# Differential attention with streamed weights: weight splits ordered behind an exponential, and two key tiles moved ahead of a hold

## The chip, the cores and the metric

One core of a Trainium2 chip runs the whole program. The metric is the device time of one execution in microseconds (us). Engines: PE (TensorE) multiplies matrices, DVE (VectorE) and ACT (ScalarE) do elementwise work, POOL (GpSimd) does small powers and issues some DMAs, SP issues the weight loads.

## The reference

The program is two transformer blocks in float32 on 1024 tokens of width 1024. The change touches one stage, the differential attention of the second block: 8 heads, each with two score maps, 64-wide queries and keys, 128-wide values, a mask that is causal by chunks of 64 tokens, and queries in blocks of 128.

```python
q = rope_partial(rms_norm(q, q_norm), cos, sin) * (ATTN_HEAD_DIM ** -0.5)
k = rope_partial(rms_norm(k, k_norm), cos, sin)
for blk in range(s // Q_BLOCK):
    q0, q1 = blk * Q_BLOCK, (blk + 1) * Q_BLOCK
    sc = jnp.einsum('bqhmd,bkhmd->bhmqk', q[:, q0:q1], k[:, :q1])
    mask = (jnp.arange(q1) // CHUNK_2)[None, :] <= (jnp.arange(q0, q1) // CHUNK_2)[:, None]
    p = jax.nn.softmax(jnp.where(mask, sc, NEG_INF), axis=-1)
    w = p[:, :, 0] - lam * p[:, :, 1]
    outs.append(jnp.einsum('bhqk,bkhd->bqhd', w, v[:, :q1]))
```

The same stage also multiplies the normed input by the key, value and query weights, and by two gate weights whose tanh goes to memory.

## The kernel before

**Precision.** Every matmul operand in float32 is split into a high and a low part (`split`, L168: an ACT copy makes the high part, a DVE subtraction the low part), and `mm3` (L171) multiplies high by high, high by low and low by high.

**Weights.** `stream` (L1150) brings one piece of weight of 128x1024: a DMA on SP into a raw buffer (a ring of 2), then the split into one of 4 pairs of buffers (`wh`, `wl`). `w2` (L1216) streams two pieces, which hold one head pair's 256 columns of the key, value or query weight. `gate_w` (L1272) streams one piece for a gate; a gate piece serves two gate units.

**Units.** The heads go in four pairs (p). A pair has 16 units (`units`, L1420), in the order of query tiles 0, 7 for one head, 0, 7 for the other, then 1, 6, then 2, 5, then 3, 4; I number them 0 to 15. The last unit of a pair, number 15, is query tile 4 of the second head. `unit_qk` (L1481) computes the scores and their two exponentials (L1522, tile `e`, recorded on the helper's line 154); `unit_mix` (L1526) combines the two maps on DVE; `unit_tr` transposes the result and splits it (`wth`, `wtl`); `unit_pv` multiplies by the values. Scores of tiles 4 to 7 need two PSUM buffers of the tag `sc`, scores of tiles 0 to 3 one; there are two such buffers.

**Fillers.** Between the units' steps the program puts work of its own that feeds later units. `fillers` (L1352) is a generator: for each pair `k_tiles` (8 key tiles and 8 value tiles), then 8 query tiles and gate units between them, and at the end two more gate units. A projected tile (`proj`, L1219) is 24 matmuls in four steps of a nominal 0.65 us, a gate unit eight such steps. `fill(us)` advances the generator until the nominal time is used; `need` (L1409) advances it until a query tile is there. A yield of a pair such as `("k", p)` is a hold: the generator stands still until the loop adds it to `done`. The hold on keys is lifted when the last unit of the pair before is the current one (L1445), the hold on values after that unit's product (L1467).

**PSUM of projections.** `proj` takes the one buffer of the tag `pj`, but inside `need` (`alone`) two of three projections take an `sc` buffer instead.

**Order on the engines.** Every engine runs its own queue in order. A compile-time scheduler writes these queues: it takes instructions by priority, which is the order in which the Python code emits them, but lets a later one go first when an engine would stand idle by the scheduler's own model of time and buffers. So fillers run earlier in the queues than their place in the code. `issue_after(ins)` adds an edge that holds only for the order: what the block emits on the engine of `ins` stands behind `ins` in that queue. Waits on data are separate.

Of the kernel before, what the change touches and what calls it, by code (L numbers as in the profile page):

```python
# [16 lines left out]
AF = mybir.ActivationFunctionType  # L17
# [112 lines left out]
class Model:  # L130
# [906 lines left out]
    def lru(self):  # L1037
        nc, A = self.nc, self.A
        D = self.dram
        self.ghb = [D.tile([128, 1024], F32, name=f"gh{i}") for i in range(8)]  # L1040
        self.tab = [D.tile([128, 1024], F32, name=f"ta{i}") for i in range(16)]
        self.x0 = None
        self.w4p = self.pool("w4")
        W = self.w4 = self.w4p.__enter__()
        self.at0p = self.pool("at0")
        self.at0 = self.at0p.__enter__()
        with self.pool("lru") as T, self.pool("m2") as M, \
# [47 lines left out]
            for c in range(8):  # L1095
# [3 lines left out]
                ps = [*proj()][1]  # L1099
# [11 lines left out]
                for g, t in ((1, ti), (0, tr)):  # L1111
                    for h in range(2):
                        z = slice(h * 512, h * 512 + 512)
                        p = PG.tile([128, 512], F32, name="pg", tag="pg")
# [84 lines left out]
    def attention(self):  # L1199
        nc, A = self.nc, self.A  # L1200
        self.ob = [self.dram.tile([128, 1024], F32, name=f"ob{i}") for i in range(8)]
        self.t0b = [self.dram.tile([128, 1024], F32, name=f"t0{i}") for i in range(8)]
        W = self.w4
        with self.pool("at1") as T1, self.pool("at") as T, \
# [8 lines left out]

            alone = [False, 0]

            def w2(src):  # L1216
                return [self.stream(W, src[j], [128, 4, 256]) for j in range(2)]

            def proj(w, i, out):  # L1219

                alone[1] = (alone[1] + 1) % 3
                if alone[0] and alone[1]:
                    p2 = PS.tile([128, 256], F32, name="pj", tag="sc")
                else:
                    p2 = PJ.tile([128, 256], F32, name="pj", tag="pj")
                q = slice(i * 128, i * 128 + 128)
                for k in range(8):
                    c = w[k // 4]
                    self.mm3(p2, (self.xnh[:, k, q], self.xnl[:, k, q]), (c[0][:, k % 4], c[1][:, k % 4]),
                             k == 0, k == 7)  # L1230
                    if k % 2:
                        yield 0.65
                c = T0.tile([128, 4, 64], F32, name="pc", tag="pc", bufs=2)
                self.act(c.rearrange("p a b -> p (a b)"), p2, AF.Copy)
                out.append(c)

            def norm_rope(ps, i, is_k):

                d = T1.tile([128, 4, 2, 64], F32, name="nr", tag="nr", bufs=3)
                sq = T0.tile([128, 4, 64], F32, name="nq", tag="nq", bufs=1)  # L1240
                self.act(sq, ps, AF.Square)
                ss = T0.tile([128, 8], F32, name="ss", tag="ss", bufs=8)
                if not is_k:
                    self.act(d, ps[:, :, None, :].to_broadcast([128, 4, 2, 64]), AF.Copy)
                nc.vector.tensor_reduce(out=ss[:, 0:4], in_=sq, op=OP.add, axis=AX.X)
                self.ts(ss[:, 0:4], ss[:, 0:4], 1.0 / 64, OP.mult, EPS, OP.add)
                self.rsqrt(ss[:, 4:8], ss[:, 0:4], 4)
                if is_k:
                    self.tt(d, ps[:, :, None, :].to_broadcast([128, 4, 2, 64]),
                            ss[:, 4:8, None, None].to_broadcast([128, 4, 2, 64]), OP.mult)  # L1250
                s = d[:, :, 0]
                r = T1.tile([128, 2, 4, 16], F32, name="rp", tag="rp", bufs=1)
                tb = rot[int(is_k)][:, i]
                for j in range(2):
                    self.tt(r[:, j].rearrange("p a (b c) -> p a b c", b=2),
                            s[:, :, None, 8 * j:8 * j + 8].to_broadcast([128, 4, 2, 8]),
                            tb[:, j:j + 1].rearrange("p a (b c) -> p a b c", b=2).to_broadcast([128, 4, 2, 8]),
                            OP.mult)
                self.tt(d[:, :, :, 0:16], r[:, 0, :, None, :].to_broadcast([128, 4, 2, 16]),
                        r[:, 1, :, None, :].to_broadcast([128, 4, 2, 16]), OP.add)  # L1260
                return d, ss[:, 4:8]
# [8 lines left out]
            gst = {}  # L1270

            def gate_w(j):  # L1272
                if j < 16 and j not in gst:
                    g, n = gates[j]
                    gst[j] = self.stream(W, A["w_gl2" if g == 0 else "w_ga2"][n], [128, 8, 128])

            def gate_unit(u):
                j, h = divmod(u, 2)
# [17 lines left out]
            WQ = {}  # L1296

            def k_tiles(p):
                wk = w2(A["w_k2"][p])
                wv = w2(A["w_v2"][p])  # L1300
                yield "k", p
                kh = T.tile([128, 4, 1024], F32R, name="kh", tag="kh")
                kl = T.tile([128, 4, 1024], F32R, name="kl", tag="kl")
                V = T.tile([128, 8, 2, 2, 128], F32R, name="V", tag="V")
                KV[p] = [kh, kl, V]
                pend = []

                def finish():
                    j, d = pend.pop(0)
                    pt = transposed(d)  # L1310
                    q = slice(j * 128, j * 128 + 128)
                    self.act(kh[:, :, q], pt, AF.Copy, scale=gcol[:, 1:2])
                    self.stt(kl[:, :, q], pt, gcol[:, 1:2], kh[:, :, q].bitcast(F32), OP.mult, OP.subtract)

                for n in range(8 + 2):
                    if n < 8:
                        o = []
                        yield from proj(wk, n, o)
                        d, _ = norm_rope(o[0], n, True)
                        pend.append((n, d))  # L1320
                    if n == 1:
                        yield "v", p
                    if n > 1:
                        j = n - 2
                        o = []
                        yield from proj(wv, j, o)
                        ps = o[0].rearrange("p (h a) b -> p h (a b)", h=2)
                        self.split(V[:, j, :, 0], V[:, j, :, 1], ps)
                        finish()
                        yield 0.3  # L1330
                        if j == 3:
                            WQ[p] = w2(A["w_q2"][p])

            def q_tile(p, i):
                o = []
# [145 lines left out]
    def unit_qk(self, unit, QS, KV):  # L1481
        nc = self.nc
        T, PS, PT, _, ma, mb, lamn, _ = self.at
        p, i, hh = unit
        self.mark(f"at{p}.{i}.{hh}")
        qs, rq = QS[p, i]
        kh, kl, _ = KV[p]
        W = (i + 1) * 128
        wc = max(W, 256)
        one = wc <= 512  # L1490
        pieces = [(0, wc)] if one else [(0, wc // 2), (512, wc // 2)]
        st = T.tile([128, 8], F32, name="st", tag="st", bufs=3)
        rqh = rq[:, 2 * hh:2 * hh + 2]
        es, vs = [], []
        sc = None
        for m in range(2):
            a = 2 * hh + m
            if m == 0 or not one:
                sc = PS.tile([128, 2, 512], F32, name="sc", tag="sc")
            base = sc[:, m] if one else sc.rearrange("p a b -> p (a b)")  # L1500
            k0 = 0
            for pi, (o, n) in enumerate(pieces):
                last = pi == len(pieces) - 1
                nc.tensor.matmul(base[:, o:o + n], qs[:, a], kh[:, a, k0:k0 + n], start=True, stop=False)
                nc.tensor.matmul(base[:, o:o + n], qs[:, a], kl[:, a, k0:k0 + n], start=False, stop=not last)
                if last:

                    end = 128 if i == 0 else o + n
                    nc.tensor.matmul(base[:, end - 64:end], ma, mb, start=False, stop=True)
                k0 += n  # L1510
            if not one:
                v = sc[:, :, 0:W // 2]
                nc.vector.tensor_reduce(out=st[:, m:m + 1], in_=v, op=OP.max, axis=AX.XY)
                self.stt(st[:, m:m + 1], st[:, m:m + 1], -1.0, rqh[:, m:m + 1], OP.mult, OP.mult)
            vs.append(sc[:, m, 0:W] if one else v)
        if one:
            nc.vector.tensor_reduce(out=st[:, 0:2], in_=sc[:, :, 0:W], op=OP.max, axis=AX.X)
            self.stt(st[:, 0:2], st[:, 0:2], -1.0, rqh, OP.mult, OP.mult)
        for m in range(2):
            e = T.tile([128, 512 if one else 1024], F32, name="e", tag=f"e{m}{int(one)}", bufs=1)  # L1520
            ev = e[:, 0:W] if one else e[:, 0:W].rearrange("p (a b) -> p a b", a=2)
            self.act(ev, vs[m], AF.Exp, bias=st[:, m:m + 1], scale=rqh[:, m:m + 1], accum=st[:, 2 + m:3 + m])  # L1522
            es.append(e[:, 0:W])
        return {"st": st, "es": es, "i": i, "hh": hh, "po": None}

# [1028 lines left out]
```

## Time and profile before

| | us |
|---|---|
| median of 3 runs | 2488.14 |
| lowest, highest | 2485.55, 2493.98 |
| the profiled execution | 2485.62 |
| its span, first to last instruction | 2483.9 |

The attention stage runs from about 703 us to 1440 us of the span. Its four pairs repeat one pattern with a period of about 179.5 us; the first pair is followed here, whose last unit ends at 882 us. The profiled execution lies 2.5 us below the median; 1.7 us of it lie outside its span.

### The profile page before, as it was taken

The numbers are of one execution on the slowest core, as the hardware profiler recorded it, in microseconds if no ns is written. First come the engines' busy times: TensorE is split into PE (matmuls) and PEld (weight loads), VectorE is DVE, ScalarE is ACT, GpSimd is POOL, SyncE is SP. The second block draws the span as 40 slices with busy tenths as digits, with TensorE's granted clock in tenths as the row PEclk, the third lists the DMA queues.
The fourth block names the chain that finished last, engine by engine and source line by source line (L and its number), as shares of the span: only waits on it lengthen the run. The fifth ranks groups of instructions, "written<-read, shape, count | busy, mean of one in ns | idle before, by whom it ended". The sixth has DMA issues, their size and how long they took to land. (4 is left out here: it accounts for less than half of the span.)

```text
span 2483.9 us, 35045 instructions
## 1 busy us (share of the span) xinstructions
PE 2355.6 (95%) x13016; PEld 1936.7 (78%) x13016; DVE 1748.2 (70%) x3344; ACT 1314.5 (53%) x2102; POOL 341.5 (14%) x363
## 2 busy tenths in 40 slices
PE   8999989999999999999899899999997999999998
PEld 6888868787888898798798678887885777666765
DVE  9667767677875666666666744235667999898987
ACT  5344532445645455454445432134435888787886
POOL 1011114100021021121121100000011111111111
PEclk9999999999999999999999999999998999999999
DMA  6322353322221111110111456532267999999992
GB/s 222 99 68 67 117 179 127 123 78 84 72 77 39 64 45 42 51 52 35 56 51 40 144 199 221 176 119 77 85 244 271 368 376 373 371 372 359 368 371 66
DMA packets 103838, 394.32 MB, mean 159 GB/s; under 512 B 14129, under 2 KB 33073, under 8 KB 79089
## 3 DMA queue, kind: packets, MB, share of 16 engines
q1 hardware_dynamic: 85008, 335.18, 37.5%
q0 software_dynamic: 18656, 56.88, 7.3%
q8 instruction: 104, 1.70, 0.3%
q14 instruction: 70, 0.57, 0.1%
HBM read 339.07 MB, written 61.31 MB: 161 GB/s over the span
## 5 line engine op out<-in xcount | busy, mean ns | idle before, releaser
L166 DVE TENSOR_TENSOR wl<-raw,wh 128x1024 fp32r<-128x1024 f32 (+1 forms) x496 | 587.7, 1209 | 130.3 <-ACT wh L154 126.1
L154 ACT ACTIVATE wh<-raw 128x1024 fp32r<-128x1024 f32 (+1 forms) x496 | 512.1, 1048 | 250.0 <-PE pj L174 67.2
L173 PE MATMUL pj<-wh,xnh 128*128 128x256 f32 x768 | 222.2, 289 | 2.1 <-ACT tg L154 1.0
L175 PE MATMUL pj<-wh,xnl 128*128 128x256 f32 x768 | 217.2, 283 | 0.0
L174 PE MATMUL pj<-wl,xnh 128*128 128x256 f32 x768 | 217.0, 283 | 0.0
L175 PE MATMUL pg<-wh,xl 128*96 128x512 f32 x512 | 201.3, 393 | 1.6 <-DVE xl L166 1.6
L174 PE MATMUL pg<-wl,xh 128*96 128x512 f32 x512 | 202.6, 396 | 0.0
L173 PE MATMUL pg<-wh,xh 128*96 128x512 f32 x512 | 200.2, 400 | 0.9 <-ACT xh L154 0.9
L173 PEld LDWEIGHTS pj<-wh,xnh 128*128 128x128 f32 x768 | 145.4, 189 | 3.8 <-ACT pc L154 2.5
L174 PEld LDWEIGHTS pj<-wl,xnh 128*128 128x128 f32 x768 | 145.2, 189 | 0.0
L175 PEld LDWEIGHTS pj<-wh,xnl 128*128 128x128 f32 x768 | 145.1, 189 | 0.0
L154 ACT ACTIVATE e<-sc,st,ss 128x1024 f32<-128x1024 f32 (+7 forms) x128 | 105.7, 829 | 54.2 <-DVE st L158 42.4
L178 POOL TENSOR_TENSOR ss<-ss,mhalf 128x4 f32<-128x4 f32 (+1 forms) x68 | 72.7, 1069 | 343.5 <-DVE ss L163 318.4
L173 PE MATMUL pd<-wh,ah 128*96 128x512 f32 x248 | 98.2, 400 | 16.6 <-ACT y L154 16.6
L175 PEld LDWEIGHTS pg<-wh,xl 128*96 128x96 f32 x512 | 83.1, 162 | 38.6 <-DVE xl L166 3.2
L173 PEld LDWEIGHTS pg<-wh,xh 128*96 128x96 f32 x512 | 83.0, 162 | 33.8 <-ACT xh L154 1.3
L174 PEld LDWEIGHTS pg<-wl,xh 128*96 128x96 f32 x512 | 82.8, 162 | 32.4
L173 PE MATMUL pg<-xnh,wh 128*128 128x512 f32 x256 | 104.9, 410 | 0.4 <-ACT kv L154 0.2
L175 PE MATMUL pg<-xnh,wl 128*128 128x512 f32 x256 | 102.6, 401 | 0.0
L173 PE MATMUL pj<-xnh,wh 128*128 128x512 f32 x256 | 102.2, 400 | 0.0
L174 PE MATMUL pg<-xnl,wh 128*128 128x512 f32 x256 | 102.2, 399 | 0.0
L174 PE MATMUL pj<-xnl,wh 128*128 128x512 f32 x256 | 101.2, 396 | 0.0
(998 smaller groups left out, 6327.5 us busy)
## 6 DMA issues: line engine op xcount, KB each, us to landing
raw<-in_w_gu SPq DMA_DIRECT2D x128, 1024.0 KB, 15.3
raw<-in_w_dn SPq DMA_DIRECT2D x64, 1024.0 KB, 15.9
raw<-in_w_out SPq DMA_DIRECT2D x16, 512.0 KB, 4.6
ta<-tg POOLq DMA_DIRECT2D x32, 256.0 KB, 2.5
t<-ta SPq DMA_DIRECT2D x14, 512.0 KB, 3.9
raw<-in_w_ga SPq DMA_DIRECT2D x12, 512.0 KB, 3.7
raw<-in_w_v SPq DMA_DIRECT2D x12, 512.0 KB, 3.5
xraw<-in_xT SPq DMA_DIRECT2D x8, 512.0 KB, 5.8
```

The source lines that it names most:

```text
L154: return self.nc.scalar.activation(out=out, in_=in_, func=func, **kw)
L166: return (eng or self.nc.vector).tensor_tensor(out=out, in0=a, in1=b, op=op)
L173: mm(ps, l[0], r[0], start=start, stop=False)
L174: mm(ps, l[0], r[1], start=False, stop=False)
L175: return mm(ps, l[1], r[0], start=False, stop=stop)
L178: self.nc.gpsimd.tensor_tensor(out=out, in0=in_, in1=self.mhalf[:, :w], op=OP.pow)
```

## The change

`unit_qk` keeps the instruction of the exponential that it emitted last in `self.last_exp`. `w2` and `gate_w` stream their weights inside `issue_after` of that instruction, so that the ACT half of each split stands behind it in ACT's queue (before the first exponential there is no edge). In `k_tiles` the first two key tiles are projected, with norm and rotation, ahead of the hold `("k", p)`; the value weights are streamed behind these two tiles; the hold on values moves from behind key tile 1 to behind key tile 2.

```diff
-        self.x0 = None
+        self.x0 = self.last_exp = None
@@
+            def after_exp():
+                return self.tc.issue_after(self.last_exp.ins) if self.last_exp else nullcontext()
+
             def w2(src):
-                return [self.stream(W, src[j], [128, 4, 256]) for j in range(2)]
+                with after_exp():
+                    return [self.stream(W, src[j], [128, 4, 256]) for j in range(2)]
@@ gate_w
-                    gst[j] = self.stream(W, A["w_gl2" if g == 0 else "w_ga2"][n], [128, 8, 128])
+                    with after_exp():
+                        gst[j] = self.stream(W, A["w_gl2" if g == 0 else "w_ga2"][n], [128, 8, 128])
@@ k_tiles
                 wk = w2(A["w_k2"][p])
+                pend = []
+                def project(n):
+                    o = []
+                    yield from proj(wk, n, o)
+                    d, _ = norm_rope(o[0], n, True)
+                    pend.append((n, d))
+                yield from project(0)
+                yield from project(1)
                 wv = w2(A["w_v2"][p])
                 yield "k", p
...
-                for n in range(8 + 2):
+                for n in range(2, 8 + 2):
                     if n < 8:
-                        o = []
-                        yield from proj(wk, n, o)
-                        d, _ = norm_rope(o[0], n, True)
-                        pend.append((n, d))
-                    if n == 1:
+                        yield from project(n)
+                    if n == 2:
                         yield "v", p
...
@@ unit_qk
-            self.act(ev, vs[m], AF.Exp, bias=st[:, m:m + 1], scale=rqh[:, m:m + 1], accum=st[:, 2 + m:3 + m])
+            self.last_exp = self.act(ev, vs[m], AF.Exp, bias=st[:, m:m + 1], scale=rqh[:, m:m + 1], accum=st[:, 2 + m:3 + m])
```

## Rows read from the trace of the kernel before

**Rows 1.** The page, part 1: busy time and share of the span by engine.

```profile
PE 2355.6 (95%) x13016; PEld 1936.7 (78%) x13016; DVE 1748.2 (70%) x3344; ACT 1314.5 (53%) x2102; POOL 341.5 (14%) x363
```

**Rows 2.** Windows: stretch, length, busy PE, PEld, DVE, ACT, POOL; PE clock, DMA share, GB/s.

```profile
866.00:880.00 14.00, 9.83 (x56) 7.85 (x55) 11.46 (x32) 6.79 (x15) 1.09 (x2) 0.88 0.00 0
876.00:879.20 3.20, 3.11 (x13) 2.95 (x13) 2.46 (x11) 1.89 (x6) 1.01 (x1) 0.50 0.00 0
838.30:841.70 3.40, 3.40 (x9) 2.65 (x9) 3.01 (x10) 1.65 (x6) 0.16 (x1) 0.50 0.72 231
1044.00:1059.00 15.00, 10.85 (x58) 8.86 (x57) 11.73 (x33) 6.80 (x15) 1.07 (x2) 0.81 0.00 0
1224.00:1240.00 16.00, 11.34 (x81) 9.45 (x80) 12.32 (x35) 8.07 (x17) 2.64 (x3) 1.00 0.01 4
880.00:930.00 50.00, 50.00 (x428) 50.00 (x427) 33.59 (x89) 26.65 (x54) 12.91 (x14) 1.00 0.14 47
```

**Rows 3.** Timeline of ACT, 804 to 838 us: start, duration, instruction, idle before.

```profile
805.19 1.06 ACT L154 ACTIVATE wh<-raw 128x1024 fp32r<-128x1024 f32 x1 [1.61 <-PE pg L174]
...
823.06 1.06 ACT L154 ACTIVATE wh<-raw 128x1024 fp32r<-128x1024 f32 x1 [0.94 <-PE pj L175]
...
826.88 1.05 ACT L154 ACTIVATE wh<-raw 128x1024 fp32r<-128x1024 f32 x1
...
835.05 1.06 ACT L154 ACTIVATE wh<-raw 128x1024 fp32r<-128x1024 f32 x1 [5.91 <-PE pg L174]
836.01 0.97 ACT L154 ACTIVATE e<-sc,st,ss 128x768 f32<-128x768 f32 x1
...
837.46 0.99 ACT L154 ACTIVATE e<-sc,st,ss 128x768 f32<-128x768 f32 x1
```

**Rows 4.** Timeline of ACT, 855 to 884 us.

```profile
855.37 1.06 ACT L154 ACTIVATE wh<-raw 128x1024 fp32r<-128x1024 f32 x1
...
861.70 0.38 ACT L154 ACTIVATE pc<-pj 128x256 f32<-128x256 f32 x1
...
866.11 0.60 ACT L154 ACTIVATE wth<-pt 128x512 fp32r<-128x512 f32 x1 [2.64 <-PE pt L1538]
...
881.15 0.89 ACT L154 ACTIVATE e<-sc,st,ss 128x640 f32<-128x640 f32 x1 [1.09 <-DVE oss L166]
...
883.32 0.66 ACT L154 ACTIVATE pc<-pj 128x256 f32<-128x256 f32 x2
```

**Rows 5.** Timeline of PE, 837 to 880 us.

```profile
837.13 0.44 PE L1504 MATMUL sc<-kh,qs 128*128 128x384 f32 x1 [1.88 <-ACT e L154]
...
838.10 0.61 PE L173 MATMUL pg<-xnh,wh 128*128 128x512 f32 x1
...
857.84 0.37 PE L173 MATMUL pj<-wh,xnh 128*128 128x256 f32 x1
...
862.63 0.28 PE L173 MATMUL pj<-wh,xnh 128*128 128x256 f32 x1
...
865.35 0.28 PE L175 MATMUL pj<-wh,xnl 128*128 128x256 f32 x1
865.47 0.60 PE L1538 MATMUL pt<-ident,e 128*128 128x128 f32 x4
...
870.48 0.50 PE L1504 MATMUL sc<-kh,qs 128*128 128x512 f32 x1 [1.07 <-ACT e L154]
...
879.29 0.36 PE L173 MATMUL pj<-wh,xnh 128*128 128x256 f32 x1
```

**Rows 6.** Timeline of DVE, 855 to 884 us.

```profile
856.78 1.23 DVE L166 TENSOR_TENSOR wl<-raw,wh 128x1024 fp32r<-128x1024 f32 x1
...
862.29 0.75 DVE L158 SCALAR_TENSOR_TENSOR e<-e,st 128x512 f32<-128x512 f32 x1
...
882.62 0.88 DVE L158 SCALAR_TENSOR_TENSOR e<-e,st 128x640 f32<-128x640 f32 x1
```

**Rows 7.** DMA issues, 780 to 860 us: count, size, us from issue to landing.

```profile
raw<-in_w_v SPq DMA_DIRECT2D x2, 512.0 KB, 3.5
```

More of the change, by code (lines that the diff above doesn't have):

```diff
@@ L1305, in k_tiles @@
                 KV[p] = [kh, kl, V]
-                pend = []
                 def finish():
@@ L1313, in finish @@
                     self.stt(kl[:, :, q], pt, gcol[:, 1:2], kh[:, :, q].bitcast(F32), OP.mult, OP.subtract)
-                for n in range(8 + 2):
+                for n in range(2, 8 + 2):
                     if n < 8:
-                        o = []
-                        yield from proj(wk, n, o)
-                        d, _ = norm_rope(o[0], n, True)
-                        pend.append((n, d))
-                    if n == 1:
-                        yield "v", p
[L1323 to L1332, printed above, removed]
+                        yield from project(n)
+                    if n == 2:
+                        yield "v", p
+                    j = n - 2
+                    o = []
+                    yield from proj(wv, j, o)
+                    ps = o[0].rearrange("p (h a) b -> p h (a b)", h=2)
+                    self.split(V[:, j, :, 0], V[:, j, :, 1], ps)
+                    finish()
+                    yield 0.3
+                    if j == 3:
+                        WQ[p] = w2(A["w_q2"][p])
             def q_tile(p, i):
```

## The prediction

> **What bounds the kernel now.** I read the busy times first: PE is busy 95% of the span [rows 1], so work taken off another engine pays only where PE stands waiting for it. Then I looked for PE's pauses in the attention stage with the windows by stretch. PE is full through most of it, as in 880 to 930 [rows 2], and pauses at one place of each pair, the last 14 to 16 us before its last exponential ends: 14.00 - 9.83 = 4.2 us in the first pair, 4.2 in the second, 4.7 in the third [rows 2]. (After the fourth pair no other head pair's keys follow.) One smaller pause of 1.88 us stands before the score matmul at 837.13 [rows 5], with a twin in each pair. In two of the three pair ends the granted clock falls to 0.50, that is 1.2 in place of 2.4 GHz, for a few us, after pauses of a few us [rows 2].
>
> The timelines of ACT and PE then show why PE pauses: the fillers have run out, and the units' own chain (scores, maximum, exponential, mix, transpose, split, product) goes from engine to engine, as in the 1.07 us before 870.48 in which PE waits for an exponential to give back an `sc` buffer [rows 5]. Two key tiles of the next pair have already run, at 857.84 and at 862.63 [rows 5], and the third only starts at 879.29. The second of them is key tile 2, not 1: tile 0 is emitted in a plain `fill` and takes the one `pj` buffer, tile 1 in `need`, where the count of three gives it an `sc` buffer, and tile 2 gets `pj` again. Tile 1 waits at 879.29 for an `sc` buffer behind the last unit. So the fillers already run ahead of the hold in PE's queue. They can because the key weights are split early: four splits of 128x1024 stand on ACT at 823.06, 826.88, 835.05 and 855.37 [rows 3, 4]. The first two are the key weights, the last two the value weights: each split frees a raw buffer, and the value weight's own load goes out right behind the first of them.
>
> **Part one, the tie on the key weights.** What matters is which exponential is the latest when `w2` for the next pair's keys is emitted. The code's own budget tells. At unit 12 `need` drives the generator past the last query tile; two gate units remain, 16 steps. The fills behind it are 2.5 and 2.0 (4 and 4 steps) at unit 12, 1.9 (3 steps) at unit 13, 2.5 (4 steps) at unit 14, and one more step in the 2.0 of unit 14. Only then `k_tiles` begins, and by then `unit_qk` of unit 15 has been emitted, at the head of that iteration. So the latest exponential is the second one of unit 15, the last of the pair, which runs at 881.15 and ends at 882.04 [rows 4]. All four key and value splits go behind it. The edge is only one of order, but ACT keeps its order: tile 0's product is copied at 861.70, tile 2's, done at 865.6, only at 883.32, although ACT stood idle for 1.09 us before 881.15 [rows 4, 5].
>
> Hence key tiles 0 and 2 leave their places at 857.84 and 862.63 and wait for: the last exponential, a high split of 1.06 us [rows 4], and a low split of 1.23 us on DVE [rows 6], behind unit 15's mix, which also follows that exponential and takes 0.88 [rows 6] (cost between 0 and 0.6 more; I take 0.2). That is 2.5 us from the end of the last exponential to the first key tile. A tile is 24 matmuls at (865.35 - 862.63)/23 = 0.118 us, 2.84 us [rows 5]; the three that are done or begun before 883 are 8.5 us.
>
> **When the last exponential then ends.** Its chain gets freer. The transposes of unit 12 were ready when the mix ended at 862.29 + 0.75 = 863.04, and PE took them at 865.47, right behind tile 2 [rows 5, 6]: 2.4 us given back. The low split at 856.78 (1.23 us on DVE [rows 6]) stood ahead of unit 12's maximum: up to 1.2. Matmuls of tile 0 stood ahead of the last query tile's transposes: up to 1.9. Together 0 to 5.5 us earlier; I take 3, the first and half of the second, since these lie on parallel branches of one chain. The last exponential then ends at 879.0, the first key tile begins at 881.5, three tiles end at 890.0. Before, the same three tiles were done at 879.29 + 2.84 + about 0.9 for eight transposes between them (two groups of four of 0.60, overlapping) = 883.0, and from there PE is full until 930 [rows 2], so what is late there is late at the end. Those transposes fit into the wait in the new order. **Loss: 7.0 us a pair; bounds 4.5 (5.5 earlier) and 10.0 (nothing earlier).**
>
> **Part one, the other weights.** The value split at 835.05 waited 5.91 us for its buffer with the exponential at 836.01 queued behind it [rows 3]; without it PE's pause of 1.88 shrinks by up to 1.06. Against that stands the fourth gate piece: its split at 805.19 [rows 3] is tied behind the second exponential of unit 9, which ends at 838.45, and its gate unit begins at 838.10 [rows 5]. With that exponential 1.06 earlier, the low part comes at 837.4 + 1.06 + 1.23 = 839.7, so the gate unit's third matmul waits about 1 us. Net 0; bounds -1 and +1. The second and third gate pieces have tens of us to spare. SP's queue: the raw ring of 2 stays full with key weights until their splits, so the value weights' loads go out only then and take 3.5 us [rows 7]: first value tile about 881.5 + 3.5 + 2.3 = 887.3. Four key tiles (11.4 us) can run in the meantime, one in an `sc` buffer between the `pj` ones. So I cost it at 0, and at up to 1 us a pair if that order doesn't come out. The query weights come later still and are needed only some 40 us on.
>
> **Part two, two tiles ahead of the hold.** In emission tile 0 moves ahead by three steps, tile 1 by two, and both get the `pj` buffer, so tile 1 no longer waits for an `sc` buffer behind unit 15. With weights in time that would fill the pause. With the weights behind unit 15's exponential there is nothing to multiply: worth 0.
>
> **The clock.** Before, the stretch at 0.50 from 876 to 879.2 did in 3.2 us what takes some 1.7 at the full clock, a cost of 1.5; the second pair's window has a mean of 0.81 over 15 us, the third pair's none [rows 2]. In the new order PE lacks two tiles (5.7 us) more in that stretch and pauses just ahead of the key tiles. I take one more such drop a pair, 3.4 us at half: 1.7 us. Bounds: -1.5 (the drops of before vanish) and +5 (the lower clock through the whole emptied stretch, where some 5 us of PE work stand on the chain). That is my estimate from [rows 2]. The Trainium skill's page "TensorE: Matmul & The Clock Gate", section "What's actually happening", speaks against this change here: it says that the throttled clock is the default and activity releases it. That the clock dropped after short pauses agrees; by that rule alone the emptied stretch is the place where it would drop for longer, which is the second rival.
>
> **Sum.** 7.0 + 0 + 0 + 1.7 = 8.7 us a pair, three pairs: 26 us. On the profiled execution's 2485.62 (span 2483.9 and 1.7 around it) that is **2512 us**. The median of before is 2.5 above that execution; I forecast from the execution, and a time within that spread is right too. Low end: 4.5 with the clock's -1.5 gives 3.0 a pair, 9 in all, 2494. High end: 10.0 with the clock's +5 and half of the late value weight gives 15.5 a pair, 46 in all, 2532.
>
> **Rivals.**
> - *Faster: the latest exponential is an earlier one* (the fillers reach the keys sooner than my count, or the edge binds less). The change then does what its parts suggest: key tiles fill the pauses of 4.2 to 4.7, the clock drop of 1.5 goes, and up to 1.06 at 837: 5 to 7 us a pair, 19 in all, about 2467. It decides if the key weights are tied to an exponential of unit 12 or before, so that they are ready by 866. Against it: the count leaves no slack of five steps. Chance 0.09.
> - *Lower clock through the emptied stretch*: 7.0 + 1.7 + 5 = 13.7 a pair, 41 in all, about 2527. For it: drops already in two of three pairs. Against it: the third pair has 4.7 us of pauses and none. Chance 0.14.
> - *No change: the chain makes up for it.* Without key tiles and splits in between, the last exponential would have to end about 10 us earlier than before, at 872. For it: PE, ACT and DVE all get freer. Against it: in 866 to 880 DVE alone is busy 11.46 of 14.00 us [rows 2], of which only about 1.4 belongs to key tile 0; some 4 us there and the 5.5 above just miss it. About 2486. Chance 0.09.
> - The forecast: 0.68.
>
> **How the numbers follow.** The likeliest is the forecast, 2512. The range 2494 to 2532 holds its bounds and the lower clock, 0.82 together. A difference under 0.3% (7.5 us) can't be told from no change. Faster by more 0.09, within it 0.09, slower by more 0.82.
>
> **What the new profile would show.** ACT: no split between 820 and the last exponential of a pair, then four behind it, the value ones some 5 us later. PE: no `pj` matmul between the last gate unit and that split, a gap of 2 us or more before the first key tile; tiles 0, 1, 2 one after another. The last exponential 0 to 5.5 us earlier relative to the pair's start. The stretch from a pair's last gate unit to the key phase's end longer by about 9 us, three times, and nothing changed before 800 us. I am wrong if the splits stand ahead of unit 13's exponentials, or if `pj` matmuls fill 866 to 880.

## The result and the profile after

The changed kernel took 2526.51 us in the median (2520.53 to 2528.59), the kernel before, on the same chip, 2486.85 (2484.53 to 2493.98): a ratio of 1.0155, with a 95% interval of 1.0138 to 1.0173. The change makes the kernel 39.7 us slower. Its profiled execution took 2520.53 us, 34.9 more than that of before, and the two traces below are compared with each other.

The page of the changed kernel, head and part 1. Against [rows 1] PE has 16 us more of busy time with as many matmuls, and a share one point lower in a longer span:

```profile
span 2518.7 us, 35048 instructions
PE 2372.0 (94%) x13016; PEld 1940.5 (77%) x13016; DVE 1751.8 (70%) x3344; ACT 1312.6 (52%) x2102; POOL 339.9 (13%) x363
```

ACT in the timeline of the changed kernel, at the first exponential of the first pair, at the end of that pair, and at the first exponential of the next (columns as in [rows 3]):

```profile
758.25 0.45 ACT L154 ACTIVATE e<-sc,st,ss 128x128 f32<-128x128 f32 x1
...
837.58 1.06 ACT L154 ACTIVATE wh<-raw 128x1024 fp32r<-128x1024 f32 x1
...
875.72 0.89 ACT L154 ACTIVATE e<-sc,st,ss 128x640 f32<-128x640 f32 x1
876.51 0.19 ACT L154 ACTIVATION_READ_ACCUMULATOR e<-sc,st,ss 128x1 f32 x1
876.60 1.99 ACT L154 ACTIVATE wh<-raw 128x1024 fp32r<-128x1024 f32 x2
...
883.14 1.06 ACT L154 ACTIVATE wh<-raw 128x1024 fp32r<-128x1024 f32 x1 [3.55 <-DMA raw<-in_w_v]
885.10 1.06 ACT L154 ACTIVATE wh<-raw 128x1024 fp32r<-128x1024 f32 x1 [0.90 <-DMA raw<-in_w_v]
...
945.11 0.45 ACT L154 ACTIVATE e<-sc,st,ss 128x128 f32<-128x128 f32 x1
```

The four splits that stood between 823 and 856 [rows 3, 4] now stand behind the pair's last exponential, at 875.72: the two of the key weights at once, those of the value weights after their own loads. (The split at 837.58 is a gate piece.) These rows give the measure used below: a **pair's period**, from its first exponential to that of the next pair, here 945.11 - 758.25 = 186.9 us, and its two parts, up to the end of the last exponential (876.61) and from there on. In the same way, for the three pairs that have a next one ("before" is the first kernel, "after" the changed one):

| | period | up to the last exponential | from there on |
|---|---|---|---|
| before | 179.5, 179.2, 178.5 | 122.6, 121.5, 122.1 | 56.9, 57.7, 56.4 |
| after | 186.9, 188.1, 187.8 | 118.4, 119.1, 118.3 | 68.5, 69.0, 69.4 |
| difference | +7.4, +8.9, +9.3 | -4.2, -2.4, -3.8 | +11.6, +11.3, +13.0 |

PE of the changed kernel at the same place. It waits for the units' chain, and its first key matmul comes only at 877.70; the second, which needs the low half of the weight, at 879.70:

```profile
861.76 0.63 PE L1550 MATMUL pt<-ident,e 128*128 128x128 f32 x4 [1.33 <-DVE e L158]
...
866.46 0.50 PE L1516 MATMUL sc<-kh,qs 128*128 128x512 f32 x1 [1.34 <-ACT e L154]
...
871.21 0.77 PE L1550 MATMUL pt<-ident,e 128*128 128x128 f32 x5 [2.47 <-DVE e L158]
...
877.70 0.58 PE L173 MATMUL pj<-wh,xnh 128*128 128x256 f32 x1
879.13 0.58 PE L1562 MATMUL po<-V,wth 128*128 128x256 f32 x1 [0.85 <-ACT wth L154]
879.70 0.58 PE L174 MATMUL pj<-wl,xnh 128*128 128x256 f32 x1
```

Windows of the changed kernel (columns as in [rows 2]): the last 14 us before the last exponential's end, the stretch at the lower clock, and what follows:

```profile
862.60:876.60 14.00, 9.64 (x53) 7.81 (x53) 10.14 (x29) 7.59 (x18) 2.11 (x2) 0.84 0.00 0
872.20:882.30 10.10, 8.72 (x37) 7.40 (x36) 8.75 (x22) 5.81 (x11) 0.60 (x1) 0.50 0.21 73
879.00:930.00 51.00, 50.87 (x418) 50.59 (x419) 34.46 (x87) 22.93 (x47) 13.46 (x14) 0.97 0.24 78
```

From 879 PE is full again, as it was in 880 to 930 [rows 2], so what is late there stays late. The expert stage begins 27.0 us later than before (first transpose of gathered rows in each trace; before first):

```profile
1881.90 1.38 PE L2232 MATMUL pt<-ident,xg 96*128 96x96 f32 x7 [6.19 <-DMA xg<-x3d,lsti]
```

```profile
1908.88 1.38 PE L2244 MATMUL pt<-ident,xg 96*128 96x96 f32 x7 [5.61 <-DMA xg<-x3d,lsti]
```

From there to the end of the span it is 602.0 us before and 2518.7 - 1908.9 = 609.8 after: another 7.8, in a stage whose code the change doesn't touch.

### The profile page after: what moved, and what is told of

The parts are those of the page before. It is cut to its first block, busy times and chain, and to the rows that moved or that the text cites. A ratio compares the mean times of both kernels' runs of the same rounds, so it can differ in the third digit from the quotient of the medians.

```text
span 2518.7 us, 35048 instructions
## 1 busy us (share of the span) xinstructions
PE 2372.0 (94%) x13016; PEld 1940.5 (77%) x13016; DVE 1751.8 (70%) x3344; ACT 1312.6 (52%) x2102; POOL 339.9 (13%) x363
## 5 line engine op out<-in xcount | busy, mean ns | idle before, releaser
L154 ACT ACTIVATE pc<-pj 128x256 f32<-128x256 f32 x96 | 36.4, 382 | 127.4 <-PE pj L175 115.4
```

The lines of the kernel that those rows point to most:

```text
L154: return self.nc.scalar.activation(out=out, in_=in_, func=func, **kw)
```

## The experiments

The experiments ran in three batches. In each the kernel before ran beside the others, with medians of 2487.57, 2487.35 and 2488.29 us, and the ratios are to it. From e2 on part two is in (the two key tiles ahead of the hold), unless it is said otherwise.

**One part alone.** The diffs stand against the changed kernel. e1 has the ties and the old `k_tiles`; e2 has part two and no tie:

```diff
             def after_exp():
-                return self.tc.issue_after(self.last_exp.ins) if self.last_exp else nullcontext()
+                return nullcontext()
```

> The kernel before with part one alone: key, value, query and gate weights tied behind the latest exponential; the key tiles stay behind the hold. Theory (the tie on the key weights costs everything, because it is the last exponential of the pair): nearly the whole loss of the changed kernel's attention stage, 24 to 30 us more than before, about 2514; no pj matmul between the last gate unit and the split behind unit 15's exponential. Rival (moving the two tiles ahead of the hold, all three into the one pj buffer, is what costs): within 5 us of before.

> Part two alone: two key tiles ahead of the hold and value weights behind them, no tie at all. Theory: key tiles 0, 1 and 2 run before the last exponential in the pj buffer, a tile of 2.84 us fills part of the 4.2 to 4.7 us of pauses, and a clock drop goes in some pairs: 3 to 6 us a pair less, 9 to 18 us faster than before, about 2474. Rival (the two tiles hurt): slower than before by 5 us or more.

e1: 2519.37 us, ratio 1.0117 (1.0101 to 1.0132), periods 187.1, 187.9, 187.5. The ties alone give the whole loss of the attention stage, and part two adds nothing to them. e2: 2482.25 us, ratio 0.9976 (0.9964 to 0.9987), periods 176.8, 175.2, 176.8: part two by itself shortens each pair, by 2.7, 4.0 and 1.7 us, less in all than expected. PE in e2 is nearly full at the pair's end (second line; the third line is the same window of the kernel before), but the stall at 836 stays, with its clock (first line):

```profile
836.00:842.00 6.00, 4.12 (x15) 3.08 (x15) 3.88 (x10) 4.79 (x10) 0.60 (x1) 0.76 0.40 129
860.00:882.00 22.00, 21.36 (x170) 19.82 (x169) 17.59 (x56) 10.75 (x26) 4.05 (x4) 1.00 0.07 23
```

```profile
860.00:882.00 22.00, 17.83 (x124) 15.85 (x124) 15.82 (x48) 10.60 (x24) 2.63 (x3) 0.92 0.04 14
```

In the second pair of e2 the stall is there too, but the clock doesn't fall. Windows of its first two periods show what that is worth:

```profile
760.31:937.12 176.81, 172.05 (x1193) 155.05 (x1192) 114.82 (x299) 88.89 (x188) 28.70 (x33) 0.99 0.14 49
937.12:1112.36 175.24, 170.49 (x1193) 153.87 (x1192) 114.66 (x299) 88.88 (x187) 28.50 (x32) 1.00 0.15 49
```

PE's pauses are the same, 176.81 - 172.05 = 4.8 us and 4.8; the 3.4 us at a granted clock of 0.50 in the first period show as 1.6 us more of busy time.

**The ties one by one.** e4 ties the key weights alone, e3 the gate weights alone, e9 the value weights alone, all to the latest exponential:

```diff
-            def w2(src):
-                with after_exp():
+            def w2(src, tie=nullcontext):
+                with tie():
...
-                wk = w2(A["w_k2"][p])
+                wk = w2(A["w_k2"][p], after_exp)   # e4; e9: on w_v2; e3: in gate_w alone
```

> Part two and the tie on the key weights alone; value, query and gate weights are not tied. Theory: the same loss as the full change, 24 to 30 us more than before, about 2514, since the value weights' loads queue behind the key weights' raw buffers anyway. Rival (the value or gate ties share the loss): less than 18 us more than before.

> Part two and the ties on the gate weights alone; key, value and query weights are not tied. Theory: the gate ties cost at most 1 us a pair, four pairs, so it lands between part two alone and 4 us above it. Rival (the gate ties carry a good part of the loss, since the fourth gate piece is needed just when unit 9's exponential ends): 8 us or more above part two alone.

> Part two, and of the ties only that of the value weights, to the latest exponential (second of unit 15); key and gate weights are free. Theory (only the key weights' place behind the last exponential costs; the value weights have the four key tiles, 11.4 us, to arrive behind): 0 to 2 us a pair slower than part two alone or up to 3 faster, since the split that waited 5.91 us ahead of an exponential at 836 is gone: 2473 to 2488. Rival (value weights behind the last exponential come too late for the first value tile): 4 us a pair or more over part two alone, over 2494.

| | us | ratio (interval) | periods |
|---|---|---|---|
| e4, key | 2505.52 | 1.0065 (1.0050 to 1.0081) | 186.0, 186.3, 187.3 |
| e3, gate | 2485.72 | 0.9997 (0.9987 to 1.0006) | 179.4, 179.5, 176.9 |
| e9, value | 2490.93 | 1.0012 (0.9998 to 1.0026) | 178.9, 179.3, 178.9 |

The key tie carries most of the loss of the attention stage: 22.4 of the 25.6 us by which the three periods of the changed kernel are longer. (In the whole time e4 lost 18.0 us, less than the 24 to 30 expected; its expert stage was shorter, see below.) The other two are not free: against e2 the gate ties cost 2.6, 4.3 and 0.1 us a pair, the value tie 2.1, 4.1 and 2.1. No run ties the query weights alone. In e3 the timeline of ACT shows what the gate ties move (four splits in three rows: two gate pieces, at 801.65 and first of the two at 836.44, and the two of the key weights):

```profile
801.65 1.06 ACT L154 ACTIVATE wh<-raw 128x1024 fp32r<-128x1024 f32 x1
836.44 2.00 ACT L154 ACTIVATE wh<-raw 128x1024 fp32r<-128x1024 f32 x2
844.18 1.06 ACT L154 ACTIVATE wh<-raw 128x1024 fp32r<-128x1024 f32 x1 [2.05 <-DMA raw<-in_w_k]
```

The gate piece's split, tied to 836, keeps its raw buffer until then, and the ring has two. The first key split stands beside it, and the second half of the key weights is loaded only after these: its split is at 844.18, not at 826.88 [rows 3]. A tie on one weight thus delays the next one through the ring. That this delay is what e3 loses is not shown: PE's pauses in its first pair add up to 7.4 us, 2.6 more than in e2, but none that the profile names waits for a key weight. The first key tile waits 0.38 us, behind a gate's tanh (`tg`):

```profile
839.59 0.88 PE L1549 MATMUL pt<-ident,e 128*128 128x128 f32 x6 [1.31 <-DVE e L158]
...
857.76 0.39 PE L173 MATMUL pj<-wh,xnh 128*128 128x256 f32 x1 [0.38 <-ACT tg L154]
```

e9, at 2490.93, lies between its theory and its rival. The timelines of PE and then of ACT show the cost:

```profile
874.51 1.33 PE L1550 MATMUL pt<-ident,e 128*128 128x128 f32 x5 [3.73 <-DVE e L158]
```

```profile
880.53 1.99 ACT L154 ACTIVATE wh<-raw 128x1024 fp32r<-128x1024 f32 x2
```

Three key tiles run early; the next in order is the first value tile, and its weights are split only at 880.53, so PE has nothing to fill the chain's pause of 3.73 us with. Against e2 the part behind the last exponential is 3.5 to 3.8 us longer in each pair; the part ahead of it is 1.4 shorter in two of them.

**The place of the tie.** The key weights alone are tied, to an exponential further back, of unit 13 (e6) and unit 11 (e7); e8 does so with the value weights alone and unit 11:

```diff
-            def after_exp():
-                return self.tc.issue_after(self.last_exp.ins) if self.last_exp else nullcontext()
+            def after_exp(back):      # self.exps: the second exponential of every unit so far
+                return self.tc.issue_after(self.exps[-1 - back].ins) if self.exps and back >= 0 else nullcontext()
...
-            def w2(src):
-                with after_exp():
+            def w2(src, back=-1):
+                with after_exp(back):
...
-                    with after_exp():
+                    with after_exp(-1):
                         gst[j] = self.stream(W, A["w_gl2" if g == 0 else "w_ga2"][n], [128, 8, 128])
...
-                wk = w2(A["w_k2"][p])
+                wk = w2(A["w_k2"][p], 2)   # e7: 4; e8: 4, on w_v2 alone
```

> Part two, and of the ties only that of the key weights, moved from the latest exponential (second of unit 15) to the second of unit 13, two units earlier. Theory (the loss is set by the point in ACT's order behind which the key splits stand): the splits run some 12 to 16 us earlier than with the full tie, the key tiles fill most of the stretch in which PE pauses, and the loss of 6.5 to 8.8 us a pair falls to between -1 and +2.5 against the kernel before: 2482 to 2496. Rival (it is the tie as such, splits that don't run early, or part two's new buffers): near the key tie's 2505.

> Part two, and the key weights tied to the second exponential of unit 11, four units before the latest. Theory: the splits then come before PE runs out of fillers, so the tie costs nothing and may bring back the exponentials' order: about the time of part two alone (2482), 2479 to 2487, with no pause over 1 us at the pair's end. Rival (the tie as such costs): over 2490.

> Part two, with the key weights free and only the value weights tied, to the second exponential of unit 11. With part two alone the first value split waited 5.91 us for its buffer at 835.88 with an exponential queued behind it, and PE paused for 1.88 us and dropped its clock there. Theory: without that wait the pause and the drop go, 1 to 2.5 us a pair: 2474 to 2482. Rival (the chain at that place is set by the vector engine or by the gate piece's low part): no gain over part two alone, 2482 to 2486.

| tie | us | ratio (interval) | periods |
|---|---|---|---|
| key, unit 15 (e4) | 2505.52 | 1.0065 (1.0050 to 1.0081) | 186.0, 186.3, 187.3 |
| key, unit 13 (e6) | 2482.92 | 0.9983 (0.9973 to 0.9992) | 176.5, 177.5, 178.6 |
| key, unit 11 (e7) | 2476.22 | 0.9955 (0.9941 to 0.9968) | 173.5, 173.3, 173.9 |
| value, unit 11 (e8) | 2475.08 | 0.9949 (0.9935 to 0.9962) | 174.2, 174.2, 174.2 |

With part two in it, the tie costs 7.5 us a pair at unit 15 against the kernel before, and gains 1.5 at unit 13 and 5.5 at unit 11. Against part two alone (e2) the tie itself costs 10.3 and 1.3 and gains 2.7. So it is not the tie as such that costs, but the place in ACT's order behind which the splits then stand. (One period says little below some 1.5 us: in e10 below, with the order of the kernel before, the second pair took 180.7 us instead of 179.2, with 10.2 us at the lower clock instead of 6.8.) In e6 the key splits stand at 863.90:

```profile
863.90 2.00 ACT L154 ACTIVATE wh<-raw 128x1024 fp32r<-128x1024 f32 x2
```

e7 and e8 beat both kernels, e7 by more than was expected (part two's 2.8 us a pair is in both). In both, the value split that waited 5.91 us at 835.05 with an exponential behind it [rows 3] is gone from there: windows of e7, then of e8, beside those of e2 above:

```profile
836.00:842.00 6.00, 5.40 (x26) 3.95 (x26) 3.60 (x14) 3.96 (x9) 0.60 (x1) 1.00 0.11 44
860.00:882.00 22.00, 20.30 (x159) 18.68 (x158) 18.69 (x58) 10.94 (x26) 4.05 (x4) 1.00 0.11 38
```

```profile
836.00:842.00 6.00, 5.15 (x27) 3.83 (x26) 3.71 (x10) 3.96 (x9) 0.60 (x1) 1.00 0.11 44
860.00:882.00 22.00, 21.37 (x170) 19.81 (x169) 17.63 (x57) 11.02 (x27) 4.05 (x4) 1.00 0.01 3
```

PE is busy 5.15 to 5.40 of the 6 us in place of 4.12, and the granted clock stays at 1.00 in place of 0.76. For e8 this is the whole gain over e2: its pauses in a pair are 3.7 us in place of 4.8, and in two of the three pairs the 1.6 us of lower clock go too. The stall at 836 is just as absent in e4, e6 and e9 (PE busy for 5.71, 6.00 and 5.64 us, clock 1.00), so it isn't what sets these apart from e7.

**The rest of the loss.** e5 is the changed kernel again; e10 and e11 are the kernel before and the changed one with 48 tiny instructions more:

```diff
             self.rotation(T1, 0)
+            zp = T1.tile([128, 4, 2], F32, name="zp", tag="zp")
+            for _ in range(16):
+                nc.vector.memset(zp[:, 0], 0.0)
+                nc.gpsimd.memset(zp[:, 1], 0.0)
+                self.act(zp[:, 2], self.ident[:, 0:2].bitcast(F32), AF.Copy)
```

> The changed kernel a second time, unchanged. In its first run the attention stage lost 27 us, and the program 39 in the median; the other 7 to 12 us come and go within the expert stage, whose instructions and their order are the same. Theory (those 7 to 12 us are variation of the transfers from execution to execution, not an effect of the change): about 2519, as the ties alone gave, with an attention stage that ends at 1464 to 1466. Rival (the change, part two together with the ties, sets the expert stage on a worse course each time): 2526 again, with the stage of the experts again 7 us longer than in the kernel before.

> The kernel before, with 16 tiny instructions (128x2) more on each of ACT, DVE and POOL at the start of the attention stage, whose results nobody reads. It is to tell why the expert stage, the same instructions in the same order, lasted 602.0 us in the kernel before, 609.8 and 610.7 in the changed one and 599.5 with the key tie alone. Theory (it varies with where the program's code lies, or from kernel to kernel for no cause in the change): the expert stage moves by 3 us or more from 602.0, with an attention stage longer by less than 4. Rival (the order that the change gives to the attention stage is behind it): 602 again, within 1.5, and 2487 to 2491.

> The changed kernel with the same 48 tiny instructions at the start of the attention stage. Theory (the expert stage varies with where the code lies): its 609.8 and 610.7 move by 3 us or more, and the time goes to between 2512 and 2524, or over 2530. Rival (the change's own doing): 610 again, within 1.5, and 2525 to 2530.

e5: 2524.81 us, ratio 1.0146 (1.0130 to 1.0163). e10: 2482.87, ratio 0.9975 (0.9960 to 0.9990). e11: 2525.53, ratio 1.0144 (1.0120 to 1.0167). The expert stage, from its first transpose to the end of the span, lasted 602.0 and 601.3 us in the two kernels with the old attention, and 609.8, 610.7 and 609.9 in the three with the changed one. My theory fell twice: the length doesn't go with the execution, and moving the code by 48 instructions doesn't shift it. In the others it was 606.5 (e1), 602.9 (e2), 599.8 (e3), 599.5 (e4), 602.5 (e6), 608.1 (e7), 605.6 (e8) and 606.0 (e9). It doesn't follow the delay either: e4 began it 21.5 us late and was the shortest, e7 13.0 us early and was among the long ones.

What I overlooked when I wrote that the order in this stage is the same: the traces have the same instructions in it (2690 matmuls on PE, and as many of each kind on ACT and DVE), but not the same order on these engines. The kernel before and e10 share one order (602.0 and 601.3 us). The changed kernel, e5 and e11 share a second (609.8, 610.7, 609.9). e1, e7 and e8 share a third (606.5, 608.1, 605.6), which e9 (606.0) has on ACT and DVE. e2, e3, e4 and e6 have one each. The timeline of PE at the first difference, in the kernel before and then in the changed one:

```profile
2178.70 0.39 PE L175 MATMUL pg<-wh,xl 128*96 128x512 f32 x1
2178.93 0.82 PE L2232 MATMUL pt<-ident,xg 96*128 96x96 f32 x8
```

```profile
2205.63 0.39 PE L175 MATMUL pg<-wh,xl 128*96 128x512 f32 x1
2206.36 0.48 PE L173 MATMUL pd<-wh,ah 128*96 128x512 f32 x1 [0.34 <-ACT y L154]
```

Windows of the stage up to there and from there on, before and then after:

```profile
1881.90:2178.70 296.80, 291.63 (x1377) 207.11 (x1378) 271.51 (x301) 246.60 (x290) 46.55 (x31) 0.99 0.99 361
2178.70:2483.90 305.20, 280.40 (x1314) 195.93 (x1312) 261.31 (x264) 239.13 (x283) 41.67 (x30) 0.99 0.85 306
```

```profile
1908.88:2205.70 296.82, 291.66 (x1378) 207.10 (x1378) 271.63 (x301) 246.46 (x291) 46.45 (x31) 0.99 0.98 361
2205.70:2518.70 313.00, 283.26 (x1314) 196.42 (x1312) 261.97 (x264) 239.29 (x283) 40.68 (x30) 0.98 0.83 298
```

Up to the same matmul the stage takes 296.8 to 297.6 us in all thirteen profiles; what differs, 302.7 to 313.1 us, stands behind it. So the 7.8 us go with another order that the scheduler wrote for a stage far behind the changed code. e1, e7 and e8 had three different attention stages, beginning the expert stage from 29.6 us late to 13.0 early, and with one order in it they stay within 2.5 us. No run sets this order on purpose, and what makes one order longer than another stays open.

e10 also sets a bound on small differences: 48 instructions that nobody needs moved the median by 0.25%, in executions other than the profiled one (2488.02 us), so where they came from is not seen. A ratio as near to 1 as those of e2, e6 and e9 says little by itself; there the periods carry the argument.

## Why the prediction came out

The predicted 2512 was the right sign and inside the range, and 26 us was two thirds of the 39.7 measured. Where the change is, in the attention stage, it was close: 27.0 us at the start of the expert stage (30.0 in e5). That the whole time lies at the second rival's 2527 is chance: this rival had 41 us in the three pairs, where 25.6 were measured.

- **Which exponential is the latest: right.** The key splits stand right behind the second exponential of unit 15 (876.60 behind 875.72). e6 and e7 show that the sign hung on this, as the rival of the faster kernel said: with part two and the key tie alone, at unit 11, the kernel gains 11 us in the whole, where that rival gave 19.
- **When the last exponential ends: right.** Forecast 3 us earlier (0 to 5.5), measured 4.2, 2.4 and 3.8. The rival in which the chain makes up for everything would have wanted about 10.
- **From there to the first key tile: about right.** Forecast 2.5 us, measured 879.70 - 876.61 = 3.1 to the first matmul with a low half.
- **The clock: the amount nearly right, the price wrong.** I expected one more drop of 3.4 us a pair. The pairs of the kernel before had 6.8, 6.8 and 3.4 us at half the clock, those of the changed kernel 10.2 each: 3.4, 3.4 and 6.8 more. It was one stretch at each pair's end (the 0.50 in the window above), so the condition of the second rival came true. But its price didn't. Three profiles of the changed order (e11's with the padding) differ in the first pair: 10.2 us at half the clock in the first of them, 6.8 in e11, 3.4 in e5, and the periods are 186.9, 186.7 and 186.4. That is some 0.5 us for 6.8 us of lower clock (the third pairs, with 10.2 in each, differ by 0.3), against the 1.7 that I put on 3.4. Where PE has no wait to take it up my price holds: 1.6 us in e2. PE's timeline of e5, at the full clock there, shows why: it stands waiting for ACT where in the other it was slower.

```profile
879.84 0.38 PE L173 MATMUL pj<-wh,xnh 128*128 128x256 f32 x1 [1.17 <-ACT wh L154]
881.27 0.38 PE L1562 MATMUL po<-V,wth 128*128 128x256 f32 x1 [1.05 <-ACT wth L154]
...
886.19 0.50 PE L173 MATMUL pj<-wh,xnh 128*128 128x256 f32 x2 [0.77 <-ACT wh L154]
```

- **The other weights: taken too low.** I took 0, with +1 for each as the bound. The changed kernel's periods are 0.9, 1.8 and 0.5 us longer than e4's, which is within the bounds together, but 3.2 us in three pairs. Two steps of the reasoning failed. I let the raw ring hold up only the value weights behind the key weights, and not the key weights behind a gate piece (e3; what this costs is not shown). And I counted four key tiles as cover for the late value weights, where the order has three and then a value tile (e9). That both cost less in the changed kernel than alone fits the late key weights hiding them, but no run shows this, nor the part of the query weights.
- **The fourth pair: left out.** With no next keys behind it, I gave it nothing. From its first exponential to the last transpose of the stage it took 143.6 us (before 140.4, e4 139.1): 3.2 us more. It was 144.4 in e2, 142.8 in e3, 141.9 in e1 and 140.1 in e9: part two alone lengthens it by 4.0, and with the key or the value tie beside it this is gone. I didn't separate this.
- **Part two: right.** Behind the late weights it was worth 0, as forecast (e1 against the changed kernel: the attention stage ends at 1465.6 and 1464.5). With weights in time it does fill the pause (e2), as the prediction also had it.
- **The sum of the three pairs: right, in part by luck.** They give 7.4 + 8.9 + 9.3 = 25.6 against the 26 forecast. In the forecast 1.7 a pair are the clock, which the runs don't show at that price; the other weights, taken at 0, come to 1.1 and make up for most of it.
- **Nothing else changes: wrong by 8 us.** The rest of the 34.9 us between the two profiled executions is 1.4 between the pairs and the expert stage (the fourth pair's 3.2, less a first exponential that came 1.2 us earlier, less some 0.5 in the stages between) and 7.8 in the expert stage, for which no step of the prediction had a place: it took the order of the later stages as given. The medians lie 39.7 apart, since the profiled execution of the changed kernel is its fastest, 6.0 below its median, and that of before 1.2 below.

## What to carry to other kernels

An order edge on an engine that keeps its order is worth what stands behind it: before tying work to "the latest" instruction of a kind, find out which one that is when the tie is made, and compare it with the time at which the first user of the tied work could run. Against the same kernel without it (e2), the edge cost 10.3 us a pair behind unit 15 and gained 2.7 four units earlier. Whoever delays one user of a ring of buffers delays the loads of whoever comes next in it. And where a scheduler writes the queues, a change can give a later stage, whose code is the same, another order: compare the orders before calling two stages the same.

## What was unexpected of the hardware

In the changed kernel the granted clock fell to 0.50 for 10.2 us behind pauses of 1.33, 1.34 and 2.47 us. In the kernel before, pauses of 4.2 us in 14 [rows 2] stood around 3.4 us of it. The same order had 10.2, 6.8 and 3.4 us of it in three profiles of its first pair, and the third pair of the kernel before, with 4.7 us of pauses at its end, none there [rows 2]. The Trainium skill's page "TensorE: Matmul & The Clock Gate", section "What's actually happening", says that the throttled clock is the default and that activity releases it. The trace agrees in that the clock fell where PE had pauses of up to 2.47 us; the 10.2, 6.8 and 3.4 us show that the pauses alone didn't tell for how long.

What the lower clock costs is decided by the chain: 1.6 us for 3.4 us of it in e2, where PE's pauses stayed the same, and some 0.5 for 6.8 in the changed order, where PE would otherwise have waited.
